# Nine of the 256 exponential units of an attention kernel computed on VectorE and GpSimd instead of ScalarE

## The chip, the cores and the metric

The kernel runs on one core of a Trainium2 chip. Its engines work side by side, each through its own queue in order: TensorE (PE; its weight loads are listed as PEld), VectorE (DVE), ScalarE (ACT), GpSimd (POOL), and SyncE (SP), which here only issues DMAs. The metric is the device time of one execution in microseconds; the time of a kernel is the median of its runs. The profile is that of one execution, and its durations are set against that execution's own time.

## The reference

Softmax attention over 8 x 8 heads, 512 queries and keys each, head dimension 64, all in fp32 at the interface:

```python
q, k, v: (8, 8, 512, 64) float32, drawn from randn
scale = 1.0 / np.sqrt(64)
scores = np.einsum('bhqd,bhkd->bhqk', q, k) * scale
scores = scores - scores.max(axis=-1, keepdims=True)
attn = np.exp(scores)
attn = attn / attn.sum(axis=-1, keepdims=True)
return np.einsum('bhqk,bhkd->bhqd', attn, v).astype(np.float32)
```

There are 64 heads x 512 x 512 exponentials. The kernel leaves the maximum out (a common factor of numerator and denominator).

## The kernel before

**Tiling.** The 64 heads are taken as 32 pairs g. Keys are cut in NI = 4 chunks c of 128. A unit (g, c, h) is the transposed score block of 128 keys by 512 queries of one head h, so there are 8 units to a pair and 256 in all. Units are grouped into score tiles st of G = 3 units (three PSUM banks; two such tiles, six banks): sizes 1, 1, 2, then 83 tiles of 3, then 2 and 1 (line 146). The other two PSUM banks are the auxiliary ring ps_x with bufs=2 (`aux`, line 105). It is shared by the transposes' tps and the attends' o; whoever asks for a third tile waits until the oldest of the two has been read.

**What happens to a pair.**
- SP loads q, k and v of a pair in 256 KB each (`load`, line 66), six pairs ahead in program order, into 7 buffers each.
- POOL casts them to fp16 (`cast_qk`, line 86; `cast_v`, line 97): q, k of pair g+3 and v of pair g+2 when pair g begins.
- PE transposes q and k (`transpose`, line 108), 8 matmuls into one auxiliary bank; DVE copies them to SBUF (line 120, tqk).
- PE computes three units of scores (`scores`, line 152), each a matmul of 64 x 128 by 64 x 512, into st.
- ACT takes the exponential of the whole tile, out of PSUM into fp16 pt (`softmax`, line 163; the activation is line 166).
- PE weighs the values with it (`weigh`, line 170, 16 matmuls of 65 columns, the 65th being the sum); this goes to an auxiliary bank o. DVE takes the reciprocal of the sums (line 187) and multiplies (line 188), SP saves the pair (`save`, line 195). Weigh, normalise and save are one `attend` (line 201) per head.

**Order.** It is written out by hand (`manual_schedule`): the order of the program is the order on each engine. The loop at line 272 goes over the score tiles, and I call one pass a stage. In stage j ACT gets tile j, PE gets the scores of tile j+1, and after that PE gets items from the queue `work`: a transpose of pair g+2 and two attends per pair. A credit of 0.42 per unit, up to 2, tells how many items a stage may take; an item costs 1. So PE's queue alternates: three scores, no to two items, three scores, and so on. The scores of tile j+1 go to the tile buffer that ACT has finished with tile j-1, so PE may start them when ACT starts tile j, and they must be there when ACT ends it.

The first head pair is brought in by a hand-written opening (lines 219 to 268), and the end is `close` (line 210).

Of the kernel before, what the change touches and what calls it, by code (L numbers as in the profile page):

```python
# [8 lines left out]

FP32 = mybir.dt.float32  # L10
FP16 = mybir.dt.float16

EXP = mybir.ActivationFunctionType.Exp
AluOp = mybir.AluOpType


@with_exitstack
def kernel(
# [4 lines left out]
    v: bass.AP,  # L23
    out: bass.AP,
):

    nc = tc.nc
    B, H, S, D = q.shape  # L30
    P = 128
    NI = S // P
    assert NI == 4 and D == 64 and S == 512
    scale = float(D) ** -0.5
    W = D + 1

    n_pairs = (B * H) // 2
    ppb = H // 2
    UPP = 2 * NI
    last = n_pairs - 1  # L40
    units = []
    for g in range(n_pairs):
        if g in (0, last):
            first = NI - 1 if g == 0 else 0
            units += [(g, (first + c) % NI, h) for h in range(2) for c in range(NI)]
        else:
            units += [(g, c, h) for c in range(NI) for h in range(2)]
    n_units = len(units)
    G = 3
    NV = 5  # L50
    AHEAD = 6
# [4 lines left out]
    ppool = ctx.enter_context(tc.tile_pool(name="att_p", bufs=8))  # L56
# [9 lines left out]
    def load(g, names="qkv"):  # L66
        if g >= n_pairs:
            return
        for nm in names:
            r = lpool.tile([P, 2, NI * D], FP32, tag=f"{nm}32", name=f"{nm}32_{g}")  # L70
            nc.sync.dma_start(out=r, in_=rows(dict(q=q, k=k, v=v)[nm], g))
            raw[g, nm] = r

    def load_head(h, nm, eng):
        if ("head", h) not in raw:
            raw["head", h] = cpool.tile([P, 2 * NI, D], FP32, name=f"raw_0_{h}")
        lo = NI * "kq".index(nm)
        eng.dma_start(
            out=raw["head", h][:, lo : lo + NI].rearrange("p (o i) d -> p o (i d)", o=1),
            in_=rows(dict(q=q, k=k)[nm], 0, h, h + 1),  # L80
        )

    vps = [cpool.tile([P, 2, NI, W], FP16, name=f"vp{n}") for n in range(NV)]
    halves, tqk, turned = {}, {}, {}

    def cast_qk(g):
        if g >= n_pairs:
            return
        qk = xpool.tile([P, 2, NI, P], FP16, tag="qk", name=f"qk_{g}")
        for n in range(2):  # L90
            nc.gpsimd.tensor_copy(  # L91
                out=qk[:, n].rearrange("p i (h d) -> p i h d", d=D),
                in_=raw[g, "qk"[n]].rearrange("p h (i d) -> p i h d", d=D),
            )
        halves[g] = qk
# [9 lines left out]
    def aux(shape, dt, name):  # L105
        return pspool.tile(shape, dt, tag="ps_x", bufs=2, name=name)

    def transpose(g, parts=(0, 1)):
        if g >= n_pairs:
            return  # L110
        if g not in turned:
            turned[g] = xpool.tile([P, 2, S], FP16, tag="tqk", name=f"tqk_{g}")
            for h in range(2):
                tqk[g, h] = [turned[g][D * h : D * (h + 1), n] for n in range(2)]
        lo, hi = parts[0], parts[-1] + 1
        ps = aux([P, hi - lo, NI, P], FP16, f"tps_{g}_{lo}")
        for n in parts:
# [7 lines left out]
    def open_cast(h, eng, lo, hi):  # L125


        if ("x", h) not in raw:
            raw["x", h] = cpool.tile([P, N, D], FP16, name=f"x_0_{h}")
            f = cpool.tile([D, NI + 1, P], FP16, name=f"t_0_{h}")  # L130
            r = cpool.tile([D, FIRST, P], FP16, name=f"r_0_{h}")
            raw["t", h] = f, r
            keys = [r[:, c] for c in range(FIRST)] + [f[:, 0]]
            tqk[0, h] = (f[:, 1:].rearrange("d n p -> d (n p)"), keys)
        eng(out=raw["x", h][:, lo:hi], in_=raw["head", h][:, lo:hi])  # L135
# [9 lines left out]

    sizes = [1, 1, 2] + [G] * ((n_units - 7) // G) + [2, 1]
    assert sum(sizes) == n_units
    firsts = [sum(sizes[:j]) for j in range(len(sizes))]
    where = {units[f + x]: (j, x) for j, (f, s) in enumerate(zip(firsts, sizes)) for x in range(s)}
    st, pt = {}, {}  # L150

    def scores(j):
        if j >= len(sizes):
            return
        if j not in st:
            st[j] = pspool.tile([P, G, S], FP32, tag="ps_st", bufs=2, name=f"st_{j}")
        for x in range(sizes[j]):
# [2 lines left out]
            key = tk[c] if g == 0 else tk[:, c * P : (c + 1) * P]  # L160
            nc.tensor.matmul(st[j][:, x, :], key, tq, start=True, stop=True)  # L161

    def softmax(j):
        n = sizes[j]
        pt[j] = ppool.tile([P, G, S], FP16, tag="pt", name=f"pt_{j}")
        nc.scalar.activation(out=pt[j][:, 0:n], in_=st[j][:, 0:n], func=EXP, scale=scale)  # L166
# [2 lines left out]

    def weigh(g, h, o, chunks, blocks=range(NI)):  # L170
        for c in chunks:
            j, x = where[g, c, h]
            for i in blocks:
                nc.tensor.matmul(  # L174
                    o[:, i, :],
                    pt[j][:, x, i * P : (i + 1) * P],
                    vps[g % NV][:, h, c, :],
                    start=(c == 0 and i == blocks[0]),
                    stop=(c == NI - 1),
                    skip_group_check=True,  # L180
                )
# [36 lines left out]
    with tc.manual_schedule():  # L218
        load_head(0, "q", nc.sync)
        load_head(0, "k", nc.scalar)  # L220
        load_head(1, "q", nc.sync)
        load_head(1, "k", nc.scalar)
        blank = cpool.tile([P, P], FP16, name="blank")
        nc.vector.memset(blank, 0.0)  # L224
        small = cpool.tile([P, 1], FP32, name="small")
        nc.vector.memset(small, 0.0)  # L226
        nc.scalar.activation(out=small, in_=small, func=EXP, scale=scale)  # L227
        ident16 = cpool.tile([P, P], FP16, name="ident16")
        make_identity(nc, ident16)
        load(1, "qk")  # L230
        load(0, "v")
        for g in range(2, AHEAD):
            load(g, "qk")
            load(g - 1, "v")
        for n in range(NV):
            nc.vector.memset(vps[n][:, :, :, D:W], 1.0)
        def busy(tile, n):
            for _ in range(n):
                nc.tensor.matmul(tile[:, G - 1, 0:P], blank, blank, start=True, stop=True)  # L239

        busy(pspool.tile([P, G, S], FP32, tag="ps_st", bufs=2, name="warm"), 24)
        A, V, Y = nc.scalar.copy, nc.vector.tensor_copy, nc.gpsimd.tensor_copy
        open_cast(0, V, 3, 6)
        open_cast(0, A, 6, 8)
        open_cast(0, A, 0, 3)
        open_cast(1, Y, 0, 3)
        a1, a2 = (aux([D, N, P], FP16, f"open_{n}") for n in range(2))
        a3 = pspool.tile([D, N, P], FP16, tag="ps_st", bufs=2, name="open_2")
        open_turn(0, 3, 6, a1)
        open_turn(0, 6, 8, a2)  # L250
        open_turn(0, 0, 3, a3)
        open_copy(0, V, 3, 6, a1)
        open_copy(0, A, 6, 8, a2)
        open_cast(1, V, 3, 8)
        open_copy(0, V, 0, 3, a3)
        st[0] = pspool.tile([P, G, S], FP32, tag="ps_st", bufs=2, name="st_0")
        busy(st[0], 4)
        scores(0)
        scores(1)
        b1, b2 = (aux([D, N, P], FP16, f"open_{n + 3}") for n in range(2))  # L260
        open_turn(1, 3, 8, b1)
        open_turn(1, 0, 3, b2)
        open_copy(1, V, 3, 8, b1)
        open_copy(1, V, 0, 3, b2)
        cast_qk(1)
        cast_v(0)
        cast_qk(2)
        cast_v(1)

        work = deque()  # L270
        credit = 0.0
        for j, n in enumerate(sizes[:-1]):
            softmax(j)
            if j > 0:
                scores(j + 1)
                if j == 2:
                    transpose(1, (0,))
                    transpose(1, (1,))
                for u in range(firsts[j - 1], firsts[j - 1] + sizes[j - 1]):
                    g, c, h = units[u]  # L280
                    r = u % UPP
                    if r == 0:
                        cast_qk(g + 3)
                        cast_v(g + 2)
                        load(g + AHEAD, "qk")
                        load(g + AHEAD - 1, "v")
                    if r == (5 if g == 0 else 2) and g + 2 < n_pairs:
                        work.append((transpose, g + 2))
                    if c == (FIRST - 1 if g == 0 else NI - 1):
                        work.append((attend, g, h))  # L290
            credit = min(credit + 0.42 * n, 2.0)
            while work and (credit >= 1.0 or j > len(sizes) - 6):
                f, *a = work.popleft()
                f(*a)
                credit -= 1.0
        while work:
            f, *a = work.popleft()
            f(*a)
        close()
# [30 lines left out]
```

The softmax here doesn't subtract the row's maximum and nothing guards it: scores larger than these inputs give would overflow.

## Time and profile before

| what | value |
|---|---|
| median of 13 runs | 127.08 us (126.29 to 130.93) |
| the profiled execution: time | 126.81 us |
| the profiled execution: span | 125.0 us (the other 1.8 us lie around it) |
| granted PE clock | 1.0 throughout |
| first score activation begins, last operation of DVE begins | 5.8 us, 121.7 us |
| HBM read and written | 25.17 MB, 8.39 MB |

The profile gives busy time and share of the span per engine, then the chain of work that ended last, then groups of instructions: source line, engine, operation, output <- inputs, their shapes and types, count, busy time and the mean duration of one, and after the second bar the time that the engine stood idle just before them, with what ended it. In the list of waits each line reads: who waited, for whom, and then the total, the number of times and the longest. The timeline has the start, the duration and the operation. Neighbouring instructions on one engine can overlap in the listing, since an instruction's listed end contains the time that its last results take; so what one costs its engine is read from start to start.

### The profile page before, as it was taken

What the parts mean: (1) busy time and instruction counts of PE and PEld (TensorE: products, weight loads), DVE (VectorE), ACT (ScalarE), POOL (GpSimd) and SP (SyncE); (2) the same over time, 40 slices, a digit from 0 to 9 for tenths busy, and PEclk for the clock granted to TensorE, in tenths of its full rate; (3) what the DMA queues carried; (4) which work ended last, traced back from release to release, by engine and by line L of the source; (5) the groups of instructions that cost most, each with busy time, mean ns of one, the idle gap of its engine ahead of it and who ended that gap; (6) DMA issues with size and microseconds to landing.
All of it is one profiled execution on the core that took longest, in us unless ns stands there. A gap on an engine that the chain in (4) does not pass through costs nothing.

```text
span 125.0 us, 3986 instructions
## 1 busy us (share of the span) xinstructions
PE 107.4 (86%) x1572; PEld 64.0 (51%) x1572; DVE 60.6 (49%) x173; ACT 117.5 (94%) x93; POOL 58.7 (47%) x101
## 2 busy tenths in 40 slices
PE   6999979889997987999798798979979898997780
PEld 6636545455564454565455265545536455554450
DVE  0344536553552645545454554645546563553450
ACT  4499999999999999999999999999999999999970
POOL 2288768475655374375456533635553554000000
PEclk9999999999999999999999999999999999999999
DMA  4999999999997999999899699899969985222222
GB/s 125 319 362 348 349 347 373 363 373 356 355 345 219 300 279 307 266 320 352 268 303 372 191 283 308 311 282 316 375 185 275 330 291 151 89 84 87 89 78 89
DMA packets 34882, 33.81 MB, mean 270 GB/s; under 512 B 2096, under 2 KB 34864, under 8 KB 34864
## 3 DMA queue, kind: packets, MB, share of 16 engines
q1 hardware_dynamic: 34576, 33.30, 82.6%
q10 hardware_dynamic: 288, 0.26, 0.7%
q8 instruction: 12, 0.20, 0.6%
q14 instruction: 6, 0.05, 0.2%
HBM read 25.17 MB, written 8.39 MB: 268 GB/s over the span
## 4 chain that ended last, share of the span: by engine, by line
ACT 74%; issue 16%; PE 6%; DVE 1%
ACT pt L166 74%; PE warm L239 2%; PE st L161 1%; PE open L139 1%; PE o_last L174 1%; PE o L174 0%; PE st L239 0%; DVE osb L188 0%; DVE rcp L187 0%; DVE blank L224 0%; DVE small L226 0%
## 5 line engine op out<-in xcount | busy, mean ns | idle before, releaser
L166 ACT ACTIVATE pt<-st 128x1536 f16<-128x1536 f32 (+2 forms) x88 | 115.1, 1599 | 1.2 <-PE st L161 1.2
L161 PE MATMUL st<-tqk 64*128 64x512 f16 x248 | 49.6, 380 | 13.1 <-ACT pt L166 11.5
L174 PEld LDWEIGHTS <-pt 128*128 128x128 f16 x1024 | 33.8, 98 | 18.0 <-issue 17.1
L174 PE MATMUL o<-vp,pt 128*128 128x65 f16 x1008 | 38.4, 194 | 0.0
L91 POOL CAST qk<-q 128x512 f16<-128x512 f32 x31 | 19.0, 613 | 30.3 <-DMA q<-in_q_dram 20.8
L187 DVE RECIPROCAL rcp<-o 128x4 f32<-128x4 f32 x63 | 11.3, 179 | 38.8 <-PE o L174 38.8
L120 DVE COPY tqk<-tps 128x1024 f16<-128x1024 f16 (+1 forms) x32 | 21.5, 675 | 15.4 <-PE tps L119 15.4
L188 DVE TENSOR_TENSOR osb<-o,rcp 128x256 f32<-128x256 f32 x63 | 26.7, 424 | 2.2
L100 POOL CAST vp<-v 128x512 f16<-128x512 f32 x32 | 19.7, 616 | 10.5 <-DMA v<-in_v_dram 8.2
L161 PEld LDWEIGHTS <-tqk 64*128 64x128 f16 x248 | 11.6, 93 | 23.4 <-issue 14.8
L119 PEld LDWEIGHTS <-qk 128*128 128x128 f16 x248 | 13.9, 98 | 13.1 <-issue 11.0
L91 POOL CAST qk<-k 128x512 f16<-128x512 f32 x31 | 19.0, 613 | 3.4 <-DMA k<-in_k_dram 2.2
L119 PE MATMUL tps<-ident,qk 128*128 128x128 f16 x248 | 19.2, 221 | 0.0
L239 PE MATMUL warm<-blank 128*128 128x128 f16 x24 | 2.7, 313 | 1.0 <-DVE small L226 1.0
L239 PEld LDWEIGHTS <-blank 128*128 128x128 f16 x28 | 2.8, 145 | 1.2 <-DVE small L226 1.0
L227 ACT ACT_TABLE_LOAD x1 | 1.3, 1283 | 1.7 <-PEq L314 1.7
L161 PE MATMUL st<-t,r 64*128 64x512 f16 x6 | 2.0, 382 | 0.0
L144 DVE COPY t<-open 64x384 f16<-64x384 f16 (+1 forms) x2 | 0.8, 415 | 1.9 <-PE open L139 1.9
L139 PE MATMUL open<-ident,x 128*64 128x128 f16 x16 | 1.7, 268 | 0.0
L139 PEld LDWEIGHTS <-x 128*64 128x64 f16 x16 | 1.3, 139 | 0.8 <-issue 0.6
L135 POOL CAST x<-raw 128x192 f16<-128x192 f32 x1 | 0.3, 343 | 2.8 <-DMA raw<-in_k_dram 2.8
L135 DVE CAST x<-raw 128x192 f16<-128x192 f32 (+1 forms) x2 | 0.6, 284 | 2.2 <-DMA raw<-in_k_dram 2.2
(20 smaller groups left out, 6.7 us busy)
## 6 DMA issues: line engine op xcount, KB each, us to landing
v<-in_v_dram SPq DMA_DIRECT2D x32, 256.0 KB, 5.5
q<-in_q_dram SPq DMA_DIRECT2D x31, 256.0 KB, 5.3
k<-in_k_dram SPq DMA_DIRECT2D x31, 256.0 KB, 5.5
out_dram<-osb SPq DMA_DIRECT2D x31, 256.0 KB, 5.1
raw<-in_k_dram ACTq DMA_DIRECT2D x2, 128.0 KB, 2.7
raw<-in_q_dram SPq DMA_DIRECT2D x2, 128.0 KB, 2.5
out_dram<-osb SPq DMA_DIRECT2D x2, 128.0 KB, 1.7
```

The lines of the kernel that those rows point to most:

```text
L91: nc.gpsimd.tensor_copy(out=qk[:, n].rearrange("p i (h d) -> p i h d", d=D), in_=raw[g, "qk"[n]].rearrange("p h (i d) -> p i h d", d=D),)
L100: nc.gpsimd.tensor_copy(out=vps[g % NV][:, :, :, 0:D], in_=raw[g, "v"].rearrange("p h (i d) -> p h i d", d=D),)
L119: nc.tensor.transpose(ps[:, n - lo, i, :], halves[g][:, n, i, :], ident16)
L120: nc.vector.tensor_copy(out=turned[g][:, lo:hi], in_=ps)
L139: nc.tensor.transpose(ps[:, i - lo, :], raw["x", h][:, i, :], ident16)
L161: nc.tensor.matmul(st[j][:, x, :], key, tq, start=True, stop=True)
L166: nc.scalar.activation(out=pt[j][:, 0:n], in_=st[j][:, 0:n], func=EXP, scale=scale)
L174: nc.tensor.matmul(o[:, i, :], pt[j][:, x, i * P : (i + 1) * P], vps[g % NV][:, h, c, :], start=(c == 0 and i == blocks[0]), stop=(c == NI ...
L187: nc.vector.reciprocal(out=rcp[:, lo:hi], in_=o[:, lo:hi, D:W])
L188: nc.vector.tensor_tensor(out=o_sb[g][:, h, lo:hi], in0=o[:, lo:hi, 0:D], in1=rcp[:, lo:hi].broadcast_to([P, hi - lo, D]), op=AluOp.mult,)
L227: nc.scalar.activation(out=small, in_=small, func=EXP, scale=scale)
L239: nc.tensor.matmul(tile[:, G - 1, 0:P], blank, blank, start=True, stop=True)
```

## The change

One unit of each of nine pairs, (g, 0, 0) for g = 4, 7, 10, ..., 28, is taken out of the list of units. The remaining 247 make 80 full tiles instead of 83, with the same small tiles at the start and the end. The unit's score matmul goes to an auxiliary bank (sa), and its exponential is made by five instructions on DVE and one on POOL, each of 128 x 512:

1. DVE, from PSUM: n = the score in half-octaves, rounded into int8 (n ~ 2 s log2 e + a shift)
2. POOL: e = n x 2^22 + a constant, as int32. Read as fp32, that is a power of the square root of two: adding half a unit to the mantissa multiplies by the root of two where the mantissa is chosen rightly, and the next half unit carries into the exponent.
3. DVE, from PSUM and n: f = 2 s log2 e - n, the fraction
4. DVE: a = (f + P) f
5. DVE: f = (f + R) e
6. DVE: pa = (a + Q) f, in fp16; steps 4 to 6 are a cubic in f times the power.

Its order: when pair g-1 begins, the start of the unit of pair g is put at the head of `work`. As an item there it issues the matmul, n, e and f. The next three stages issue one each of steps 4, 5 and 6, ahead of the stage's items. The credit per unit is 0.46 instead of 0.42. `weigh` takes pa in place of the slice of pt. The position within a pair, r, is counted from the pair's first unit in the shortened list.

```diff
+EXP_P, EXP_Q, EXP_R = 2.28771887, 28.39494972, 3.73321451
+SHIFT = -0.8899647686
+LEAD_BITS = 1008370304
+LOG2E = 1.4426950408889634
...
+    aside = [(g, 0, 0) for g in range(4, last, 3)]
+    units = [u for u in units if u not in aside]
     n_units = len(units)
+    first_of = {g: next(n for n, u in enumerate(units) if u[0] == g) for g in range(n_pairs)}
...
+    apart = {}
+
+    def exp_aside(g):
+
+        _, c, h = unit = next(u for u in aside if u[0] == g)
+        tq, tk = tqk[g, h]
+
+        def tmp(nm, dt=FP32):
+            return ppool.tile([P, S], dt, tag=nm, bufs=2, name=f"{nm}_{g}")
+
+        n, e, f, a = tmp("n", I8), tmp("e", I32), tmp("f"), tmp("a")
+        out16 = tmp("pa", FP16)
+        s = aux([P, S], FP32, f"sa_{g}")
+        nc.tensor.matmul(s, tk[:, c * P : (c + 1) * P], tq, start=True, stop=True)
+        rate = 2.0 * scale * LOG2E
+        nc.vector.tensor_scalar(
+            out=n, in0=s, scalar1=rate, scalar2=SHIFT, op0=AluOp.mult, op1=AluOp.add
+        )
+        nc.gpsimd.tensor_scalar(
+            out=e,
+            in0=n,
+            scalar1=float(1 << 22),
+            scalar2=float(LEAD_BITS),
+            op0=AluOp.mult,
+            op1=AluOp.add,
+        )
+
+        def step(o, x, k, y, op0=AluOp.add, op1=AluOp.mult):
+            nc.vector.scalar_tensor_tensor(out=o, in0=x, scalar=k, in1=y, op0=op0, op1=op1)
+
+        step(f, s, rate, n, AluOp.mult, AluOp.subtract)
+        yield
+        step(a, f, EXP_P, f)
+        yield
+        step(f, f, EXP_R, e.bitcast(FP32))
+        yield
+        step(out16, a, EXP_Q, f)
+        apart[unit] = out16
+        yield
+
+    steps = deque()
+
+    def begin_aside(g):
+        steps.append(exp_aside(g))
+        next(steps[-1])
...
         for c in chunks:
-            j, x = where[g, c, h]
+            p = apart.get((g, c, h))
+            if p is None:
+                j, x = where[g, c, h]
+                p = pt[j][:, x]
             for i in blocks:
                 nc.tensor.matmul(
                     o[:, i, :],
-                    pt[j][:, x, i * P : (i + 1) * P],
+                    p[:, i * P : (i + 1) * P],
...
-                    r = u % UPP
+                    r = u - first_of[g]
                     if r == 0:
+                        if any(a[0] == g + 1 for a in aside):
+                            work.appendleft((begin_aside, g + 1))
                         cast_qk(g + 3)
...
-            credit = min(credit + 0.42 * n, 2.0)
+            while steps and next(steps[0], 1) == 1:
+                steps.popleft()
+            credit = min(credit + 0.46 * n, 2.0)
             while work and (credit >= 1.0 or j > len(sizes) - 6):
```

More of the change, by code (lines that the diff above doesn't have):

```diff
@@ L11 @@
 FP16 = mybir.dt.float16
+I32 = mybir.dt.int32
+I8 = mybir.dt.int8
 EXP = mybir.ActivationFunctionType.Exp
 AluOp = mybir.AluOpType
+EXP_P, EXP_Q, EXP_R = 2.28771887, 28.39494972, 3.73321451
+SHIFT = -0.8899647686
+LEAD_BITS = 1008370304
+LOG2E = 1.4426950408889634
 @with_exitstack
```

## The prediction

> **What bounds the kernel now.** I read the page's engine shares first, then the chain that ended last, the groups kept apart by shape, the waits, and last the timeline of two stretches. The page:
>
> ```profile
> PE 107.4 (86%) x1572; PEld 64.0 (51%) x1572; DVE 60.6 (49%) x173; ACT 117.5 (94%) x93; POOL 58.7 (47%) x101
> ...
> ACT 74%; issue 16%; PE 6%; DVE 1%
> ```
>
> ACT is busy 94% of the span, and the chain is ACT; its "issue" is the seam between two activations. Pieces of the chain, in order of time:
>
> ```profile
> 111.27 1.33 ACT pt L166
> ...
> 112.65 1.04 ACT pt L166
> ...
> 113.99 1.01 ACT pt L166
> ...
> 115.32 1.31 ACT pt L166
> ```
>
> The activations start 1.34 to 1.38 us apart, always. The groups give the same: 83 full tiles in 111.7 us of unioned time are 1.346 us a tile, or 0.449 us for one of its three units. (The mean of 1644 ns of one contains overlap with the next.) I call these 1.35 us a stage.
>
> ```profile
> L166 ACT ACTIVATE pt<-st 128x1536 f16<-128x1536 f32 x83 | 111.7, 1644 | 0.0
> L188 DVE TENSOR_TENSOR osb<-o,rcp 128x256 f32<-128x256 f32 x63 | 26.7, 424 | 2.2
> L120 DVE COPY tqk<-tps 128x1024 f16<-128x1024 f16 x30 | 20.7, 692 | 14.4 <-PE tps L119 14.4
> L91 POOL CAST qk<-k 128x512 f16<-128x512 f32 x31 | 19.0, 613 | 3.4 <-DMA k<-in_k_dram 2.2
> ```
>
> The waits tell who is late for whom:
>
> ```profile
> DVE rcp L187 <- PE o L174: 38.8, 43, 1.8
> ...
> PE st L161 <- ACT pt L166: 11.5, 32, 0.7
> ...
> ACT pt L166 <- PE st L161: 1.2, 2, 1.0
> ```
>
> ACT waited for PE twice, at the start; PE waited for ACT 32 times, 11.5 us. So today every stage ends on ACT, and PE is up to 0.7 us early. The next lines price PE's steps (start, duration, operation):
>
> ```profile
> 112.48 0.62 PE L119 MATMUL tps<-ident,qk 128*128 128x128 f16 x8
> ...
> 113.03 0.60 PE L161 MATMUL st<-tqk 64*128 64x512 f16 x3
> ...
> 114.37 0.59 PE L161 MATMUL st<-tqk 64*128 64x512 f16 x3 [0.73 <-ACT pt L166]
> ...
> 114.89 1.16 PE L174 MATMUL o<-vp,pt 128*128 128x65 f16 x32
> ...
> 115.97 0.60 PE L161 MATMUL st<-tqk 64*128 64x512 f16 x3
> ```
>
> From start to start: a transpose 0.55, three scores 0.52 (0.17 each), two attends 1.08. A pair costs PE 8 x 0.17 + 1.08 + 0.55 = 3.0 us, ACT 8 x 0.449 = 3.6 us. A stage's scores take 0.60 and must be there within 1.35, so PE may begin them 0.75 late before ACT feels it.
>
> **The change, part by part.**
>
> *Removed.* Nine units leave ACT: 80 full tiles instead of 83, with the same small ones at both ends. 3 x 1.346 = **-4.04 us**, all of it on the chain.
>
> *PE.* Nothing more to compute: the nine scores only go to a bank of their own (sa). Over three pairs PE needs 9.1 us and ACT 23 x 0.449 = 10.3, so by rate ACT still sets the pace. In the built order the crowded stages (three scores, two attends or a transpose and an attend) are 1.6 us, 0.26 over a stage, and the next ones are 1.06. Cost 0, hidden under ACT; without that cover it is what is late in the walk below.
>
> *DVE.* Five instructions of 128x512 per unit, 45 in all. The trace has none. Nearest rows: osb, fp32, 256 columns, one PSUM operand, 424 ns; reciprocal, 4 columns, 0.18. Slope (424-182)/252 = 0.96 ns a column, so 512 columns are 424 + 256 x 0.96 = 0.67; taking one column a cycle I use **0.69**. Ends: below, the copy of twice as many columns at 692 ns, which would be 0.42 for 512 (the two 512-column copies took 0.42); above, the same plus a whole POOL cast, 0.69 + 0.61 = 1.30. I take 0.69, being nearest to osb, the row of the same type. 45 x 0.69 = 31 us: DVE goes from 60.6 to about 92 us, 76% of the shorter span. It is not the bound by rate, but it is in order, and PE waits for it through the two auxiliary banks (tps, o, now sa too). What queues behind n, f, a is the reciprocal of an attend or the copy of a transpose, and for these banks PE waits, with the next scores behind.
>
> A walk through one of the three alignments (pairs 4, 13, 22), zero where the stage's scores start. sa follows at 0.52 and is there at 0.93 (0.38 of matmul, and the semaphore). n 0.93, f 1.65 to 2.34. The first attend's rcp and osb end at 2.90 (an independent instruction starts 0.07 before the last one's listed end: 47.29, 0.42 long, is followed at 47.64). a ends at 3.52, the second attend's osb at 4.08, f times e at 4.70, the copy of the transpose at 5.32. PE: the second attend waits for sa's bank until 2.34 instead of running at 1.87; the scores of the third stage start at 2.88, 0.18 late; the transpose runs at 3.40; scores 4.04, attend 4.56, and the next attend, wanted at 5.10, needs the transpose's bank: 5.35 to 5.89. The next scores, due at 5.38, start 0.51 late. ACT bears 0.75, so **0.24 us of margin** is left. The other two alignments give about 0.3 by the same walk. So without a surprise ACT loses nothing, but there is little to spare.
>
> The unknown is what a, f times e and the last step cost when both their tensor operands lie in SBUF while POOL works. The osb rows stay at 423 to 425 ns and the copies at 692 to 693 with POOL busy half of the time, so an instruction with a PSUM operand is not touched; n and f have one. For the other three no row exists: bounds 0 and one cast, 0.61 each. POOL is busy just then: e releases the three casts queued behind it. I take 0.15 to 0.2 each (half a cast, on somewhat more than half the occasions would be 0.18), about 0.4 to 0.5 by the time the banks are wanted; less the margin of 0.24 to 0.3 that leaves some 0.1 to 0.2 of ACT idle in the tight alignments and none in others: **0.1 us x 9 = +0.9 us**.
>
> The Trainium skill speaks against this part: the page GPSIMD Engine Reference, section Key points, says that GpSimd shares its SBUF interfaces with VectorE and contends with its instructions that have two SBUF inputs. Those are these three steps; with no contention the sum would be 4.04 us gained, with a cast's wait on every one none of it would be left.
>
> *POOL.* Nine e of 512 columns. Nearest row, the cast of 512: 0.61; ends 0.3 (the 192-column cast took 0.34) and 1.2 (two casts). I take 0.6, 5.5 us in all on an engine 47% busy. It is wanted by f times e two stages (2.7 us) after it starts, so up to 2 us it costs nothing. The same page, section Performance versus the Vector engine, has 0.77 us as measured for 512 elements at best; the cast here took 0.61. By either the sum is the same.
> The new wait of e on n holds the casts behind it. Today POOL runs about 6 us ahead of its place in the program (cast of pair 13's q at 37.9, its place after pair 10 has begun at about 43); e, emitted one pair before its unit, cuts that to some 2 us, and the transposes need the casts a pair later still. Cost 0; the loads' buffers are freed far earlier than SP asks for them, so SP's queue does not move. If that cover went, a late cast would hold PE at the transposes.
>
> *DMA.* The same bytes. Mid-span 300 to 308 GB/s, but 361 between 10 and 30 us; a pace 3.3% higher asks for some 315. Nothing.
>
> *Credit 0.42 to 0.46.* One more work item per aside; a changed interleave, counted in the walk.
>
> **Sum**, against the profiled execution (126.81 us, span 125.0): 126.81 - 4.04 + 0.9 = 123.7. That execution is 0.27 under the median of 127.08, which I carry over: **123.9 us**.
>
> **Rivals.**
> 1. *No contention.* The walk holds with its margin: 127.08 - 4.04 = 123.0. For it: constant osb durations; against: the three steps have other operands.
> 2. *The ring of two banks becomes the bound in part.* If the three steps are each 0.2 longer, the lateness grows by 0.6; over the margin of 0.24 that is 0.36 of ACT idle, in the two alignments that I take to be hit 6 x 0.36 = 2.2: 123.0 + 2.2 = 125.2. For it: sa holds a bank for 1.4 us where an attend holds it 1.3 with PE's own work, and margins are 0.24 to 0.31. Against: PE has 1.2 us of slack per three pairs to recover.
> 3. *Slower: POOL and DVE take turns.* a and f times e wait for casts in full or nearly so (0.61 + 0.3), 0.9 an aside; less 0.3 of margin, 0.6 x 9 = 5.5: 128.5. It decides from 4.04/9 = 0.45 of stall, 0.75 of lateness an aside, that is 0.25 on each of the three. For it: POOL's casts are queued exactly there. Against: POOL is idle half of the time, and only one of the three falls surely beside a cast.
> 4. *It does not do what it says*: pa comes late for its attend, and ACT's saved time goes into that wait. By the walk pa is ready about 6 us after sa. In the first alignment its attend comes more than 2 us later still; in the other two it is wanted only 0 to 0.4 us after pa ends, and there the next scores would start 0.44 to 0.47 late, with 0.28 to 0.31 of margin. So it is the same lateness on the same margin, and part of cases 2 and 3.
>
> **How the numbers follow.** Forecast (123.3 to 124.6) 0.46; no contention 0.20; the ring 0.17, of which 0.03 ends within 0.3% of before; contention 0.17, of which 0.04 within 0.3% and 0.13 slower. About 0.3% is what a measurement of this kernel can tell from no change. Faster 0.46 + 0.20 + 0.14 = 0.80, same 0.07, slower 0.13. The range goes from the full gain with 0.3 of scatter, 122.7, to the ring's price and half of the way to no change, 126.3; beyond it lie most of case 3 and little else.
>
> **What would show it.** Right: 80 full activations with an unchanged distance of 1.35; DVE near 92 us, its five steps near 0.69; ACT's idle time for PE's scores under 2 us, in the stages three to five after an sa. Wrong: a, f times e or the last step well over 0.69, or DVE gaps before them released by POOL; ACT waiting 0.45 us or more per aside; PE's attends waiting for tqk or osb; activations slowed by DVE's reads of PSUM, for which the trace has no sign.

## The result, and the profile after it

The changed kernel took **128.99 us** (median of 11 runs) against 126.98 us for the kernel before (48 runs). The ratio is 1.016, 95% interval 1.013 to 1.018: slower by 2.0 us, where 3.2 us of gain were forecast. Some executions of either kernel fall in a slower state, some per cent longer; this ratio and those below compare the others. The profiled execution took 128.34 us, with a span of 126.5 us.

The page of the changed kernel, engine shares and then the chain that ended last:

```profile
PE 107.1 (85%) x1572; PEld 64.0 (51%) x1572; DVE 93.1 (74%) x218; ACT 115.1 (91%) x90; POOL 73.1 (58%) x110
...
PE 32%; ACT 29%; DVE 26%; issue 9%; POOL 1%; ACTq 0%
```

ACT held three quarters of the chain before; now it has 29%, and PE and DVE hold the rest in turns. DVE's total is 93.1 us, close to the 92 that were forecast, so the total does not tell what went wrong. The groups do (line, engine, operation, shapes, count | busy, mean ns of one | idle time before them and its releaser):

```profile
L205 DVE SCALAR_TENSOR_TENSOR pa<-a,f 128x512 f16<-128x512 f32 x9 | 9.4, 1040 | 0.0
L205 DVE SCALAR_TENSOR_TENSOR f<-f,e 128x512 f32<-128x512 f32 x9 | 9.2, 1024 | 0.0
L205 DVE SCALAR_TENSOR_TENSOR a<-f 128x512 f32<-128x512 f32 x9 | 6.3, 699 | 0.2
L192 DVE TENSOR_SCALAR n<-sa 128x512 int8<-128x512 f32 x9 | 6.2, 691 | 2.6 <-PE sa L190 2.6
L195 POOL TENSOR_SCALAR e<-n 128x512 int32<-128x512 int8 x9 | 5.9, 657 | 30.0 <-DVE n L192 29.9
```

Three of the five steps cost what was reckoned (0.69), e too (0.66). f times e and pa cost 1.02 and 1.04; and POOL stood still 29.9 us until n came. Among the waits, PE's for ACT fell (11.5 us before), ACT's for PE rose (1.2 before), and PE's for tqk is all but new (0.3 before):

```profile
PE st L175 <- ACT pt L226: 6.1, 17, 0.7
...
ACT pt L226 <- PE st L175: 4.4, 11, 0.7
...
PE st L175 <- DVE tqk L134: 3.3, 4, 1.1
```

The list counts only gaps in which ACT is quite empty. A better measure is the distance of the starts of neighbouring full activations, which is 1.33 us in a stage without a wait, in both kernels. Summed over the steady part, what lies above 1.333 is 0.62 us before and **6.66 us** after; I call this ACT's loss. The balance: three activations less are -4.0 us, the loss is up by 6.04, together +2.0. The two profiled executions differ by 1.5 us: after the change the first full activation also starts 0.35 us earlier, and what follows the last one is 0.2 shorter. (That the medians differ by 2.0 is chance.) So the removal gave all that it could, and 0.67 us more than before was lost at each of the nine units put aside in the mean, 0.2 to 1.2 one by one.

One such place, the timeline of the changed kernel (start, duration, operation, in brackets the idle time before it and its releaser):

```profile
53.89 0.61 POOL L114 CAST vp<-v 128x512 f16<-128x512 f32 x1
53.93 1.10 DVE L205 SCALAR_TENSOR_TENSOR f<-f,e 128x512 f32<-128x512 f32 x1
...
54.45 1.06 POOL L105 CAST qk<-q 128x512 f16<-128x512 f32 x1
54.96 0.68 DVE L134 COPY tqk<-tps 128x1024 f16<-128x1024 f16 x1
55.46 0.61 POOL L105 CAST qk<-k 128x512 f16<-128x512 f32 x1
55.56 1.05 DVE L205 SCALAR_TENSOR_TENSOR pa<-a,f 128x512 f16<-128x512 f32 x1
...
55.70 0.39 PE L175 MATMUL st<-tqk 64*128 64x512 f16 x1 [1.15 <-DVE tqk L134]
...
56.18 1.45 ACT L226 ACTIVATE pt<-st 128x1536 f16<-128x1536 f32 x1 [0.73 <-PE st L175]
```

f times e starts just after a cast has begun and takes 0.4 us longer; the next cast starts while f times e runs and takes 1.06 instead of 0.61; while DVE copies tqk out of PSUM, POOL goes on; the next cast starts, and pa comes just behind it. The engines take turns, and who starts first decides: 16 of the 18 f times e and pa start 0.04 to 0.10 us after a cast, and each then lasts until 0.47 us after that cast's start plus its own 0.68. The step a reads f twice, so its operands too lie in SBUF; in six of the nine places it starts 0.01 us ahead of a cast, and the cast waits instead:

```profile
31.02 0.69 DVE L205 SCALAR_TENSOR_TENSOR a<-f 128x512 f32<-128x512 f32 x1
31.03 1.16 POOL L105 CAST qk<-q 128x512 f16<-128x512 f32 x1
```

In the place shown first, the third unit of the next scores reads the very tqk that stands behind f times e: PE waits 1.15 us for it, ACT 0.73 for PE.

### The profile page after: what moved, and what is told of

The parts are those of the page before. It is cut to its first block, busy times and chain, and to the rows that moved or that the text cites. A ratio compares the mean times of both kernels' runs of the same rounds, so it can differ in the third digit from the quotient of the medians.

```text
span 126.5 us, 4034 instructions
## 1 busy us (share of the span) xinstructions
PE 107.1 (85%) x1572; PEld 64.0 (51%) x1572; DVE 93.1 (74%) x218; ACT 115.1 (91%) x90; POOL 73.1 (58%) x110
## 4 chain that ended last, share of the span: by engine, by line
PE 32%; ACT 29%; DVE 26%; issue 9%; POOL 1%; ACTq 0%
ACT pt L226 29%; PE st L175 13%; PE o L237 10%; DVE osb L251 7%; DVE f L205 5%; PE tps L133 4%; DVE pa L205 3%; DVE a L205 3%; DVE tqk L134 3%; DVE n L192 3%; DVE rcp L250 2%; PE warm L302 2%; PE open L153 1%; POOL qk L105 1%; PE o_last L237 1%
## 5 line engine op out<-in xcount | busy, mean ns | idle before, releaser
L226 ACT ACTIVATE pt<-st 128x1536 f16<-128x1536 f32 (+2 forms) x85 | 112.7, 1435 | 5.0 <-PE st L175 4.4
L105 POOL CAST qk<-q 128x512 f16<-128x512 f32 x31 | 25.0, 806 | 3.1 <-DMA q<-in_q_dram 2.0
L114 POOL CAST vp<-v 128x512 f16<-128x512 f32 x32 | 24.6, 770 | 1.1 <-DMA v<-in_v_dram 0.4
L195 POOL TENSOR_SCALAR e<-n 128x512 int32<-128x512 int8 x9 | 5.9, 657 | 30.0 <-DVE n L192 29.9
L205 DVE SCALAR_TENSOR_TENSOR pa<-a,f 128x512 f16<-128x512 f32 x9 | 9.4, 1040 | 0.0
L205 DVE SCALAR_TENSOR_TENSOR f<-f,e 128x512 f32<-128x512 f32 x9 | 9.2, 1024 | 0.0
L192 DVE TENSOR_SCALAR n<-sa 128x512 int8<-128x512 f32 x9 | 6.2, 691 | 2.6 <-PE sa L190 2.6
L205 DVE SCALAR_TENSOR_TENSOR f<-sa,n 128x512 f32<-128x512 f32 x9 | 6.2, 691 | 0.3
L205 DVE SCALAR_TENSOR_TENSOR a<-f 128x512 f32<-128x512 f32 x9 | 6.3, 699 | 0.2
L237 PE MATMUL o<-vp,pa 128*128 128x65 f16 x36 | 2.7, 196 | 2.6 <-DVE osb L251 1.9
```

The lines of the kernel that those rows point to most:

```text
L105: nc.gpsimd.tensor_copy(out=qk[:, n].rearrange("p i (h d) -> p i h d", d=D), in_=raw[g, "qk"[n]].rearrange("p h (i d) -> p i h d", d=D),)
L114: nc.gpsimd.tensor_copy(out=vps[g % NV][:, :, :, 0:D], in_=raw[g, "v"].rearrange("p h (i d) -> p h i d", d=D),)
L192: nc.vector.tensor_scalar(out=n, in0=s, scalar1=rate, scalar2=SHIFT, op0=AluOp.mult, op1=AluOp.add)
L195: nc.gpsimd.tensor_scalar(out=e, in0=n, scalar1=float(1 << 22), scalar2=float(LEAD_BITS), op0=AluOp.mult, op1=AluOp.add,)
L205: nc.vector.scalar_tensor_tensor(out=o, in0=x, scalar=k, in1=y, op0=op0, op1=op1)
L237: nc.tensor.matmul(o[:, i, :], p[:, i * P : (i + 1) * P], vps[g % NV][:, h, c, :], start=(c == 0 and i == blocks[0]), stop=(c == NI - 1), ...
```

## The experiments

Theory C: contention; DVE's steps whose tensor operands both lie in SBUF and POOL's casts take turns, and DVE, late, makes PE late. Rivals: B, the five steps' place in DVE's queue is enough without contention; P, the casts held behind e come late; L, the attend waits for pa. The experiments added J, the late copy of a transpose, and R, the steps' place ahead of an attend's normalisation.

### Casts left out

```diff
     def cast_qk(g):
         if g >= n_pairs:
             return
+        if g >= 8:
+            halves[g] = halves[g - 4]
+            return
...
     def cast_v(g):
-        if g >= n_pairs:
+        if g >= NV:
             return
```

> The changed kernel with POOL's casts left out from pair 8 on (v from pair 5 on): the transposes and attends read the casts of earlier pairs, so the output is that of other data; loads, PE, ACT and DVE do the same work, and POOL does only e. Theory C (f times e and pa wait for POOL's casts, because an instruction of DVE with two different SBUF operands and one of POOL take turns; in the changed kernel they took 1.06 and 1.10 us, a and n 0.69): both fall to 0.69, ACT's waits fall from 0.74 us an aside to 0.1 or less, and the time is 123.0 to 124.0. Rival B (the five steps stand ahead of the reciprocals on DVE and that is enough, contention or not): the two steps fall to 0.69, but ACT still waits 0.4 us or more an aside, 126.5 to 128. Rival P (POOL stands still behind e until n comes, 29.9 us in all, and the transposes get late casts): as C in time, so the run without e must tell these apart.

125.85 us, ratio 0.992 (0.989 to 0.995). The steps fell to 0.68 (one pa, while casts still ran, took 1.05). Neither C (123 to 124) nor B (126.5 to 128) had the time right. ACT's timeline of this run (idle time in brackets) says why; I read it from 32 us on, since the granted PE clock fell to a half for some microseconds before that:

```profile
32.14 25.63 ACT L229 ACTIVATE pt<-st 128x1536 f16<-128x1536 f32 x19 [0.85 <-PE st L178]
58.14 1.45 ACT L229 ACTIVATE pt<-st 128x1536 f16<-128x1536 f32 x1 [0.37 <-PE st L178]
59.76 29.66 ACT L229 ACTIVATE pt<-st 128x1536 f16<-128x1536 f32 x22 [0.17 <-PE st L178]
89.79 1.45 ACT L229 ACTIVATE pt<-st 128x1536 f16<-128x1536 f32 x1 [0.37 <-PE st L178]
91.42 18.91 ACT L229 ACTIVATE pt<-st 128x1536 f16<-128x1536 f32 x14 [0.17 <-PE st L178]
```

The waits are gone in two of three alignments, as the prediction's walk has them; in the third (pairs 13 and 22 here) ACT still loses 0.85 to 0.97 us, and PE waits there for tqk:

```profile
56.47 0.39 PE L178 MATMUL st<-tqk 64*128 64x512 f16 x2
...
57.51 0.68 DVE L208 SCALAR_TENSOR_TENSOR pa<-a,f 128x512 f16<-128x512 f32 x1
57.65 0.09 PEld L178 LDWEIGHTS <-tqk 64*128 64x128 f16 x1 [1.08 <-DVE tqk L137]
57.65 0.39 PE L178 MATMUL st<-tqk 64*128 64x512 f16 x1 [0.79 <-DVE tqk L137]
```

So there is a second cause that needs no contention: J.

### The same without the change

The same edit on the kernel before.

> Control: the kernel before with the same casts left out (output of other data). Casts were nowhere on its path, so every theory expects 126.5 to 127.3; were it faster, the time of the changed kernel without casts would have to be read against it.

Ratio 1.0005 (0.998 to 1.003). The casts are off its path.

### Without e

```diff
-        nc.gpsimd.tensor_scalar(
-            out=e,
-            in0=n,
...
-        step(f, f, EXP_R, e.bitcast(FP32))
+        step(f, f, EXP_R, e_const)
```

> The changed kernel without POOL's e: f times e reads a constant tile that is filled once at the start (the power is left out, so the nine units weigh wrongly). POOL is never held by n and its casts again run ahead; DVE has its five steps as before, beside casts that now fall at random. Rival P (held casts): the gain appears, 123 to 124.5. Theory C: the casts are still there, about half of POOL's time; the two steps come down from 1.06 and 1.10 to 0.8 to 0.95, and the time to 125 to 127.5. Rival B: 128 to 129.

128.49 us, ratio 1.011 (1.004 to 1.019). POOL ran ahead again, and P's gain did not come: P falls as a main cause. The casts now began in no fixed order with the steps, and `a` was hit as well where a cast had begun first:

```profile
31.43 0.61 POOL L105 CAST qk<-q 128x512 f16<-128x512 f32 x1 [0.77 <-PE st L175]
31.53 1.07 DVE L198 SCALAR_TENSOR_TENSOR a<-f 128x512 f32<-128x512 f32 x1
```

a, f times e and pa took 0.82, 0.86 and 0.82 in the mean. That is 0.43 us of lateness an aside (over 0.69 each) against 0.69 in the changed kernel, and a loss of 5.84 us against 6.66. The time is 1 us above what I had expected of C, since I did not yet know of J: its three places alone lost 3.8 of the 5.84 us.

### Another unit

```diff
-    aside = [(g, 0, 0) for g in range(4, last, 3)]
+    aside = [(g, NI - 1, 1) for g in range(4, last, 3)]
```

(and the second attend is queued after the last unit that is left.)

> The changed kernel with unit (g, 3, 1) aside instead of (g, 0, 0): pa is now the last chunk of the pair's second attend instead of the first of its first, more than 3 us later. A rival of its own, L (PE's attend waits for pa itself, which the changed kernel shows 5 times, 2.8 us): 126 to 127. Theory C (the waits come by way of the two banks, pa's wait is their symptom): 128 to 129.5, with ACT's waits for scores still 0.6 us or more an aside.

Ratio 1.016 (1.009 to 1.022), loss 7.3 us: no gain from taking L's wait away. So L alone does not make the change lose; what it costs there is not told apart, since J's places lost more in this run (up to 2.6 us, there in part at a lower granted PE clock).

### The transposes first

```diff
-                        work.append((transpose, g + 2))
+                        work.appendleft((transpose, g + 2))
```

> The changed kernel with a transpose put at the head of the queue of work instead of its end. Theory J (in one of the three alignments, pairs 4, 13 and 22, the copy of a transpose stands behind three of the five steps on DVE, and the very next scores read it; without casts this alignment alone still cost 0.8 to 0.9 us an aside): the waits of these three asides, 1.05 us each, come down to what contention leaves, 0.3 to 0.7; the other six stay at 0.65; the time is 127 to 128.3. Without J: 128.7 to 129.3, the three waits unchanged.

133.84 us, ratio 1.049 (1.046 to 1.052): far off. The copy's wait went, but a new one came:

```profile
PEld L237 <- DVE pa L205: 7.9, 6, 2.4
...
PE o L237 <- DVE pa L205: 5.4, 3, 1.9
```

In the alignment of pairs 10, 19 and 28 the transpose now also goes ahead of sa, and the attend that reads pa comes three stages after sa instead of four. L, whose removal gained nothing in the changed kernel, became the largest wait here.

### Both: transposes first, casts left out

> Both edits: casts left out from pair 8 on (output of other data, as in the first run) and the transposes first. If contention and the late copy are all of it, ACT's waits are gone but for 0.05 an aside, and the full gain of three activations appears: 122.8 to 123.6. If something third holds ACT (the two banks alone), 124.5 or more.

126.36 us, ratio 0.995 (0.993 to 0.998), where 122.8 to 123.6 was expected. In the alignment of J every distance is 1.33 to 1.35 now, but for pair 4, where casts still run: J is shown. The loss of 3.95 us lies, but for 0.5 at pair 4, in the three places (1.0 to 1.2 us each) where the attend waits for pa: L, as in the run before.

### Half casts

```diff
-            nc.gpsimd.tensor_copy(
-                out=qk[:, n].rearrange("p i (h d) -> p i h d", d=D),
-                in_=raw[g, "qk"[n]].rearrange("p h (i d) -> p i h d", d=D),
-            )
+            for b in range(2):
+                nc.gpsimd.tensor_copy(
+                    out=qk[:, n, :, b * D : (b + 1) * D],
+                    in_=raw[g, "qk"[n]][:, b].rearrange("p (i d) -> p i d", d=D),
+                )
```

(v likewise.)

> The changed kernel with each of POOL's casts cut in two of 256 columns, one for each head; nothing else. Theory C as turns by whole instructions (DVE's step waits for the end of the cast that runs): f times e and pa wait for half as long a piece, 0.85 to 0.95 us instead of 1.06 and 1.10, and the time falls by 1 to 2 us, 127 to 128. If the two engines share element by element, the steps stay at 1.05 to 1.1 and the time at 128.5 to 129.5.

**125.87 us**, ratio 0.994 (0.991 to 0.998): with this alone the change is a gain. It did more than expected, the two steps are back at 0.71 and 0.73:

```profile
L207 DVE SCALAR_TENSOR_TENSOR pa<-a,f 128x512 f16<-128x512 f32 x9 | 6.5, 727 | 0.0
L207 DVE SCALAR_TENSOR_TENSOR f<-f,e 128x512 f32<-128x512 f32 x9 | 6.4, 710 | 0.4 <-POOL e L197 0.4
```

The traces show why. In all runs, a step with both operands in SBUF that finds a POOL instruction of 512 columns begun (0.03 us or more before) starts its own 0.68 us only 0.47 us after that instruction's start (0.468 to 0.477); with 256 columns it is 0.26 us (0.256 to 0.264). A step that comes later than that does not wait. Here the steps find a half begun 0.08 us or more before and wait 0 to 0.18 us, where whole casts made f times e and pa wait 0.37 to 0.43. The same place as above, in this kernel:

```profile
53.53 0.68 DVE L207 SCALAR_TENSOR_TENSOR f<-f,e 128x512 f32<-128x512 f32 x1
53.62 1.20 POOL L116 CAST vp<-v 128x256 f16<-128x256 f32 x2
...
54.87 0.39 PE L177 MATMUL st<-tqk 64*128 64x512 f16 x1 [0.96 <-DVE tqk L136]
55.36 1.45 ACT L228 ACTIVATE pt<-st 128x1536 f16<-128x1536 f32 x1 [0.54 <-PE st L177]
```

Now POOL is the one that waits (two halves take 1.20 beside the step, 0.74 alone), and POOL, busy for 70% of the span, has time. J is still there, and most of the remaining loss of 3.85 us is in its three places.

> Control: the kernel before with POOL's casts cut in two of 256 columns. No DVE instruction there has two SBUF tensors and casts are not on its path: every theory expects no change, 126.4 to 127.2. A gain here would mean that the 125.9 us of the changed kernel with half casts come from the casts themselves and not from the turns that the engines take.

The control, the same edit on the kernel before: ratio 0.999 (0.997 to 1.002). The gain is not the casts' own.

### fp16 steps, transposes first

```diff
-        n, e, f, a = tmp("n", I8), tmp("e", I32), tmp("f"), tmp("a")
+        n, e, f, a = tmp("n", I8), tmp("e", I16), tmp("f", FP16), tmp("a", FP16)
```

(and the power with steps of 512 on 16 bits.)

> The transposes first, and f, a, the power and the product in fp16 (e as int16 with half-octaves of 512): the three steps with SBUF operands read and write 16 bits. If DVE runs them at two columns a cycle, as it does the copies of 1024 fp16 columns in 0.69, they take 0.42 plus the wait for a cast, 0.4 us less each, and the time is 124 to 126, below both kernels. If they stay at one column a cycle, 127 to 128.3 as with the transposes alone.

A miss. Its four runs took 136.6 to 142.3 us, too scattered for a ratio, so only its durations are used: the shortest of the steps with all operands in fp16 is 0.676 us, as in fp32, so the type shortens none of them. `a` now found a cast begun 0.11 us before in six of nine places and took 1.05.

### Taking the three waits away together

> Three edits on the changed kernel: half casts, the transposes first, and unit (g, 3, 1) aside, so that pa is the last chunk wanted. If the three waits found so far (DVE's steps for a cast, scores for a late copy, the attend for pa) are all of it, ACT waits 0.1 us or less an aside and the time is 122.8 to 123.6, 3% below the kernel before. If the ring of two banks has a price of its own, 124 to 125.

124.66 us, ratio 0.979 (0.970 to 0.989).

> The same without the half casts: whole casts, the transposes first, unit (g, 3, 1). Contention alone is left. If it only matters by way of the late copy and the late pa, 123 to 124; if its 0.7 to 0.8 us an aside reach ACT by the banks as well, 125 to 127; were the late copy and pa not the cause of the 133.8 us of the transposes-first run, 130 or more.

128.41 us, ratio 1.012 (1.009 to 1.015), loss 6.2 us. Between these two only the casts' length differs: with the late copy and the late pa both gone, contention still costs 3.2% of the kernel before (1.012 to 0.979), 4.1 us, give or take 1.2 by the intervals (the losses in the two traces, 6.2 and 2.5, say 3.7), and by the banks:

```profile
PEld L237 <- DVE osb L251: 7.1, 11, 1.0
...
PE o L237 <- DVE osb L251: 4.0, 8, 0.9
```

> Half casts and the transposes first, with unit (g, 0, 0) as in the changed kernel. The transposes-first run (133.8) lost 1.9 us in each of its three worst places, where the attend waited for pa up to 2.4 us; without casts that wait was 1.2 to 1.7 us at most and the time 126.4. If contention only adds to that wait, half casts give 126 to 127; the three worst places stay, 0.9 to 1.2 us each.

127.07 us, ratio 0.998 (0.992 to 1.004). Here PE waits for pa 5 times as its weights and 3 times as the matmul's: with unit (g, 0, 0) the transposes first bring L back, whatever the casts.

### What was left

The kernel of three edits lost 2.5 us, 0.7 to 0.9 in each of three places, where an attend waits for a bank whose osb stands behind f times e:

```profile
76.79 0.67 PE L239 MATMUL o<-vp,pt 128*128 128x65 f16 x16 [0.45 <-DVE osb L253]
...
78.09 2.79 ACT L228 ACTIVATE pt<-st 128x1536 f16<-128x1536 f32 x2 [0.31 <-PE st L177]
```

```diff
-            while steps and next(steps[0], 1) == 1:
-                steps.popleft()
             credit = min(credit + 0.46 * n, 2.0)
             while work and (credit >= 1.0 or j > len(sizes) - 6):
                 f, *a = work.popleft()
                 f(*a)
                 credit -= 1.0
+            while begun and steps and next(steps[0], 1) == 1:
+                steps.popleft()
+            begun = bool(steps)
```

> Half casts, the transposes first, unit (g, 3, 1), and each of the later steps a, f times e and pa after the stage's items instead of ahead of them, so that an attend's reciprocal and product are not behind them on DVE. Theory R (what is left in the kernel of the three edits, 0.7 us in one of three alignments, is an attend waiting for a bank whose osb stands behind f times e): these three waits fall to 0.2 or less, 122.6 to 123.6. Rival (n and f hold the bank, the place of the later steps is nothing): 124.3 to 125.

**123.27 us**, ratio 0.971 (0.967 to 0.975): 2.9% faster than the kernel before and the fastest of all. R is shown: the three losses fell from 0.9, 0.7 and 0.7 us to 0.5, 0.1 and 0.15, though the first stays above the 0.2 expected. ACT's loss is 0.8 us over the steady part, about what the kernel before has (0.62), and ACT holds the chain again:

```profile
ACT 69%; issue 18%; PE 10%; DVE 1%
```

> The transposes first and unit (g, 3, 1), with POOL's casts left out from pair 8 on (output of other data). If half casts had taken all of the contention away, this is no faster than the three edits with half casts, 124 to 125, with the same 0.7 us in one of three alignments. If half casts still cost by POOL (its casts are longer and wait for DVE, and a late cast holds a transpose), 122.8 to 123.8.

Its four runs scatter from 124.6 to 128.6 us, so only the distances in its trace count: the three places still lose 1.0, 0.7 and 0.7 us without any casts. What was left is not contention.

## Why the prediction was wrong

**Right.** ACT's gain (4.04 us forecast, 4.0 found; the last version shows nearly all of it as time), the price of n and f (0.69) and of e (0.6 forecast, 0.66), PE's rate. That POOL's hold behind e costs little is borne out by the run without e. DVE's total agrees by luck: one by one the 45 steps take 37.3 us, 6 more than the 31 reckoned, but neighbours overlap in the listing and the total grew by 32.5. That a took 0.70 is luck too: it starts 0.01 us ahead of a cast. (The upper end of the range, 126.3, would be 126.1 by its own words.)

**The term that failed: the three steps beside POOL.** It was put at 0.15 to 0.2 each, "half a cast, on somewhat more than half the occasions", because POOL is idle half of the time. Measured: 0 on a, 0.33 to 0.35 on f times e and pa in the mean, 0.7 us an aside. The bounds (0 and 0.61) held. What was wrong is to take POOL's idle half as spread evenly. The change itself moves it: POOL now idles *before* e (29.9 us), and the casts behind e find their data landed (their waits for DMAs fell from 31 us to 3). So POOL runs on without a pause just while the steps run, and 16 of 18 f times e and pa found a cast just begun. A wait that is added to one queue sets when that engine's other work falls. The Trainium skill's rule that spoke against the change (GPSIMD Engine Reference, section Key points) was borne out, with 0.37 to 0.43 us for each meeting of these two steps.

**The step that was missing: whom the copy serves.** The walk let the copy of the transpose end at 5.32 and asked only when its bank was wanted. But in that alignment the scores due at 4.04 read it: their third unit could not start before 5.35. That was 1 us late, with 0.75 allowed; "0.24 us of margin" was none, even without contention (0.85 to 0.97 us lost without casts).

**The allowance of 0.75 us was too large.** In the run without casts, at 56.47, the scores end 0.97 us late (58.04 instead of 56.47 + 0.60), ACT starts 0.10 after that, and 0.56 us is lost: 0.41 was to spare. Of a stage's 1.33 us, some 0.20 also pass between ACT's start and that of the scores and 0.10 between their end and ACT's next start, which the 0.75 leaves out. The next scores stand behind two attends that began late, and lose 0.29 more. The other two alignments lost nothing without casts, as forecast, but with less to spare than the 0.3 stated.

**The rivals.** The slower one (128.5) was the right mechanism, though it named a and f times e where f times e and pa were hit; by its break-even 0.45 us of stall per aside decides, and it was 0.67. Its chance of 0.17 was too small, because it was weighed by POOL's mean share. Its size was put on contention alone: by the ratios contention costs 2.7 us (half casts alone, 1.016 to 0.994) to 4.1. In the trace of the changed kernel J's three places lost 3.1 us and the other six 3.5; without casts J's places still lose and the others do not. These do not add up neatly, since each removes part of what another would have hidden: moving the transposes first alone made it 133.8, and the other unit alone gained nothing.

**Left open.** That the first to start goes first is read from starts and lengths in the traces; no run set the order of the starts by itself, and why a cast lets DVE go some 0.14 us before its listed end is not known. The halves of the casts of v and of q and k were not told apart, nor the 0.5 us that the last version still loses in its first place.

## What to carry to other kernels

Before work goes to an idle engine, look at when that engine and its neighbours would be busy *after* the change, not at their mean shares: a wait added to an in-order queue gathers the work behind it into one burst, and here the burst met the very steps that it was to serve. In a hand-made order, follow each delayed instruction to all its readers, its data's as well as its buffer's; of the four waits here, taking one away brought another to the front. Where two engines take turns by whole instructions, cutting the less urgent one's instructions in two can turn a loss into a gain by itself: 1.016 became 0.994 by one edit.

## What the runs showed of the hardware

- A DVE step with both tensor operands in SBUF and a POOL cast lengthen each other (0.68 to 1.10, 0.61 to 1.06 us): the later one waits. It makes no difference whether the operands are two tensors or one read twice (a: 0.69 where it began 0.01 us ahead of a cast, 1.05 to 1.10 where a cast had begun 0.05 to 0.11 before).
- DVE's wait ends 0.47 us after the start of a POOL instruction of 512 columns (listed at 0.61) and 0.26 after that of a cast of 256 (listed at 0.40), in every trace that has such a meeting.
- DVE's instructions with a PSUM operand are not touched (osb 423 to 426 ns, n and f 680 to 693 throughout).
- With casts of 256 columns f times e and pa have a median of 0.68 us and a mean of 0.71 and 0.73 in the changed kernel (0.76 and 0.82 at most; a 0.86), and it is mostly POOL that waits.
- The scalar-tensor-tensor step of 512 columns takes 0.68 us in fp32 and in fp16 alike.
